# The gate products of a PEER layer: a scaled one-hot in two parts, two products a token

## The chip, the cores and the metric

The kernel runs on one core of one Trainium2 chip. The metric is the device time of one execution in microseconds (us). Three runs of the kernel before gave 2240.7, 2244.51 and 2245.97 us; their median, 2244.51 us, is the time to compare with. The execution that the profiler recorded took 2239.97 us.

## The reference

Two transformer blocks in fp32 follow each other: a hybrid mixer with a PEER feed-forward layer, then layers with attention and SwiGLU. The change touches the PEER layer alone. For each of 256 tokens and each of 8 heads it scores two sets of 128 sub-keys, takes the 16 best of each, adds them in pairs, keeps the 16 best sums, and reads from them 16 expert numbers out of 128 x 128 and 16 gates (a softmax). The result for a token is a sum over its 8 x 16 = 128 chosen experts:

```
u = w_down[ib]
act = gelu(einsum("td,thkd->thk", xb, u)) * gb
v = w_up[ib]
y = einsum("thk,thkd->td", act, v)
```

## The kernel before, in words

The kernel doesn't gather experts. It computes all 16384 of them for all 256 tokens and multiplies by a gate that is zero for experts that were not chosen. The experts stand as 128 rows (the first index) of 128 experts (the second index, on the partitions). For each row `r_` the loop in `peer` (from L963) multiplies 8 tiles of the down weights with the activations. Every weight tile and every activation is split into a high and a low part in fp32r, so a tile takes three one-pass products (`mm3`, L315 to L317): 24 products of 256 columns a row. The split of the weights runs on the way: ScalarE writes the high part wH (L288), and VectorE or, for every second group of four tiles, GpSimd writes the low part wL (L294). `self.share = 0.5` sets that half.

`value` puts the gelu of a row into `buf[:, r, n:]` (L957) for tokens whose gates are not there yet; for the first n tokens, which have their gates, it multiplies at once (L960, then L961 on GpSimd for odd rows and on VectorE for even ones).

`route` (a generator that the loop steps through) finds the experts of 128 tokens on VectorE. It ends with three transposes; `sel` then holds for each token the two indices of its 128 (head, choice) pairs on the partitions, and `gsel` their gates (L921, L922).

From row 60 on, each row also takes a group of four tokens. `onehot` (L928) builds, for both indices of the four tokens, one-hot matrices of 128 x 128 (L931, one VectorE instruction of 1024 columns, written over the tile `h`, which is parked in DRAM meanwhile) and scales the first of them by the gates: in one group of four by one VectorE instruction of 512 columns (L933), in the other three by four ScalarE instructions of 128 columns (L936). `gates` (L938) multiplies the two one-hots of each token in fp32 on TensorE (L943), which gives that token's 128 x 128 table of gates. The four tables lie interleaved in one PSUM bank (the token index is innermost). VectorE multiplies the rows that exist already into `buf` (L945), ScalarE copies the rest there (L947), where later rows find it. There are 64 groups, in rows 60 to 124.

Two buffers of one-hots (`oh[g % 2]`) let `onehot` run up to two groups ahead of the products. Within an engine the order of instructions is set by a planner that follows priorities and estimated durations, not by hand; semaphores carry what one engine needs of another.

After the 128 rows, the loop from L1001 multiplies with the up weights (L999); at `r == 4` of it the parked `h` comes back by DMA (L1013, L1014) and a factor `rn` of the next norm is computed (L1020).

Of the kernel before, what the change touches and what calls it, by code (L numbers as in the profile page):

```python
# [8 lines left out]
F32 = mybir.dt.float32  # L9
F32R = mybir.dt.float32r  # L10
I32 = mybir.dt.int32
U32 = mybir.dt.uint32
AF = mybir.ActivationFunctionType
ALU = mybir.AluOpType
# [4 lines left out]
P = 128  # L19
D = 1024  # L20
KD = D // P
S = 256
M = 16
T = M + S
# [183 lines left out]
class Net:  # L208
    def __init__(self, tc, ctx, I, out, dump=None):
        self.tc, self.nc, self.I, self.out = tc, tc.nc, I, out  # L210
        self.dump = dump or (lambda name, ap: None)
        nc = self.nc
        self.per = ctx.enter_context(tc.tile_pool(name="per", bufs=1))
        self.wp = ctx.enter_context(tc.tile_pool(name="wp", bufs=1))
        self.tp = ctx.enter_context(tc.tile_pool(name="tp", bufs=1))
        self.dr = ctx.enter_context(tc.tile_pool(name="dr", bufs=1, space=DRAM))
        per = self.per
        self.vecs = per.tile([P, NVEC], F32, name="vecs")
        nc.sync.dma_start(out=self.vecs[:, :KD], in_=I["vecs"][:, :KD])
        self.cst = per.tile([P, 7 * P], F32, name="cst")  # L220
        self.ident = self.cst[:, :P]
        self.tri = self.cst[:, P : 2 * P]
        self.tris = self.cst[:, 2 * P : 3 * P]
        self.blk = self.cst[:, 3 * P : 4 * P]
        self.iota = self.cst[:, 6 * P : 7 * P]
        self.band2 = self.cst[:, 4 * P + 64 : 4 * P + 64 + 32]
        self.band1 = self.cst[:, 5 * P : 5 * P + 31]
        self.halfm = self.cst[:, 5 * P + 64 : 5 * P + 66]
        self.ones = per.tile([P, P], F32, name="ones")
        nc.vector.memset(self.ones, 1.0)  # L230
        self.eps = {}
        for e in (1e-5, 1e-6):
            t = per.tile([P, 1], F32, name="eps%d" % len(self.eps))
            nc.vector.memset(t, e)
            self.eps[e] = t
        warm = per.tile([P, 1], F32, name="warm")
        nc.scalar.activation(out=warm, in_=self.eps[1e-5], func=AF.Sqrt)
        self.h = per.tile([P, KD, T], F32, name="h")
        self.uH = per.tile([P, KD, T], F32R, name="uH")
        self.uL = per.tile([P, KD, T], F32R, name="uL")  # L240
        self.nchunk = I["wall"].shape[0]
        self.raw = {}
        self.hl = {}
        self.loaded = 0
        self.split = 0
        self.pos = 0
        self.turn = 0.0
        self.share = 0.0
        self.factor = None
        self.over = ExitStack()  # L250
        self.later = []

    def behind(self, eng):

        return self.tc.issue_after(next(i for i in reversed(self.nc.cur_bb.bb.instructions) if i.engine == eng.engine))

    def vec(self, name, i=0, n=1):
        o, _ = VEC[name]
        return self.vecs[:, o + i : o + i + n]
# [536 lines left out]
    def peer(self):  # L796


        nc = self.nc
        h = self.h  # L800
        NT = P
        with ExitStack() as ctx:
            pool = ctx.enter_context(self.tc.tile_pool(name="pr", bufs=1))
            buf = pool.tile([P, NT, S], F32, name="buf")
            hd_ = self.dr.tile([P, KD, S], F32, name="hd")
            sel = pool.tile([P, S, 2], F32, name="sel")
            gsel = pool.tile([P, S], F32, name="gsel")

            rows = lambda a, b: buf[:, a:b].rearrange("p a b -> p (a b)")
            sc = rows(112, 128).rearrange("p (t m k) -> p t m k", t=2, k=P)  # L810
# [36 lines left out]
            for d in range(KD):  # L847
                t = self.t_("t", 2)[:, :S]
# [20 lines left out]
            def route(tt):  # L869
# [7 lines left out]
                for dst, src in ((cand, v), (cidx, fi)):  # L877
                    o = 0
                    for r0, r1, n in ((0, 1, 16), (1, 2, 8), (2, 4, 5), (4, 8, 3), (8, 16, 1)):
                        k = r1 - r0  # L880
                        nc.vector.tensor_tensor(
                            out=dst[:, :, o : o + k * n].rearrange("p h (a b) -> p h a b", b=n),
                            in0=src[:, :, 0, r0:r1, None].to_broadcast([P, 8, k, n]),
                            in1=src[:, :, 1, None, :n].to_broadcast([P, 8, k, n]), op=ALU.add)
# [31 lines left out]
                ts = slice(tt * P, (tt + 1) * P)  # L916
                p2 = self.bank("ax")
                nc.tensor.transpose(p2[:, :128], e[:, :128], self.ident)
                nc.tensor.transpose(p2[:, 128:256], e[:, 128:256], self.ident)
                nc.tensor.transpose(p2[:, 256:384], tv.rearrange("p h j -> p (h j)"), self.ident)  # L920
                nc.vector.tensor_copy(out=sel[:, ts].rearrange("p t i -> p i t"), in_=p2[:, :256].rearrange("p (i t) -> p i t", i=2))  # L921
                nc.vector.tensor_copy(out=gsel[:, ts], in_=p2[:, 256:384])  # L922
                yield

            flat = h.rearrange("p d t -> p (d t)")
            oh = [flat[:, 1024 * i : 1024 * (i + 1)].rearrange("p (t w k) -> p t w k", w=2, k=P) for i in range(2)]

            def onehot(g):  # L928
                o = oh[g % 2]
                ts = slice(4 * g, 4 * g + 4)  # L930
                nc.vector.tensor_tensor(out=o, in0=self.iota[:, None, None, :].to_broadcast([P, 4, 2, P]), in1=sel[:, ts, :, None].to_broadcast([P, 4, 2, P]), op=ALU.is_equal)  # L931
                if g % 4 == 0:
                    nc.vector.tensor_tensor(out=o[:, :, 0], in0=o[:, :, 0], in1=gsel[:, ts, None].to_broadcast([P, 4, P]), op=ALU.mult)  # L933
                else:
                    for t in range(4):
                        nc.scalar.activation(out=o[:, t, 0], in_=o[:, t, 0], func=AF.Copy, scale=gsel[:, 4 * g + t : 4 * g + t + 1])  # L936

            def gates(g, R):  # L938

                o = oh[g % 2]  # L940
                ps = self.bank("acc").rearrange("p (i t) -> p i t", t=4)
                for t in range(4):
                    nc.tensor.matmul(ps[:, :, t], o[:, t, 1], o[:, t, 0], start=True, stop=True)  # L943
                ts = slice(4 * g, 4 * g + 4)
                nc.vector.tensor_tensor(out=buf[:, :R, ts], in0=ps[:, :R], in1=buf[:, :R, ts], op=ALU.mult)  # L945
                if R < NT:
                    nc.scalar.activation(out=buf[:, R:, ts], in_=ps[:, R:], func=AF.Copy)  # L947

            pace = 0.0
            work = [x for tt in range(2) for x in [route(tt)]]  # L950
            done = 0
            pend = -1
# [35 lines left out]
            def act(r):  # L988
                i = r % LAST if r < N0 else LAST + r - N0
                t = self.uH[:, i, M:], self.uL[:, i, M:]  # L990
                self.hilo(*t, buf[:, r])
                acts[r] = t

            def add(r, d):
                H, L = self.wtile()
                o = y[d // 2][:, (d % 2) * S : (d % 2 + 1) * S]
                aH, aL = acts[r]
                for i, (a, b) in enumerate(((H, aH), (H, aL), (L, aH))):
                    nc.tensor.matmul(o, a, b, start=(r == 0 and d % 2 == 0 and i == 0), stop=(r == NT - 1 and i == 2), skip_group_check=True)  # L999
                return o  # L1000
# [4 lines left out]
            for r in range(N0):  # L1005
                if r + 2 < N0:
                    act(r + 2)
                if N0 - 3 * LAST <= r < N0 and (N0 - r) % 3 == 0:
                    act(NT - (N0 - r) // 3)
                for d in range(KD):  # L1010
                    add(r, d)
                if r == 4:
                    nc.scalar.dma_start(out=h[:, :, M:], in_=hd_)  # L1013
                    nc.scalar.dma_start(out=h[:, :, :M], in_=self.I["mt2"])  # L1014
                    w2 = pool.tile([P, KD], F32, name="w2")
                    nc.vector.tensor_tensor(out=w2, in0=self.vec("norm_fin", 0, KD), in1=self.vec("ln_ffn1_0", 0, KD), op=ALU.mult)
                    self.norm_begin("ln_ffn1_0", 0, M)
                    for d in range(KD):
                        self.norm_tile(d)
                    rn = self.norm_end(1e-6, self.t_("rnext", 1))  # L1020

# [5 lines left out]
            for d in range(KD):  # L1029
                for r in range(N0, NT):  # L1030
                    ps = add(r, d)
                o = h[:, d, M:]
# [554 lines left out]
```

## Time and profile before

| what | value |
|---|---|
| median of three runs | 2244.51 us |
| the profiled execution | 2239.97 us |
| span of its instructions | 2238.0 us |
| mean granted TensorE clock | 0.995 of full |
| TensorE busy (matmul rows) | 2169.0 us, 97% |
| VectorE busy | 1590.4 us, 71% |
| ScalarE busy | 1323.0 us, 59% |
| GpSimd busy | 671.7 us, 30% |

The span runs from the first instruction to the last; some 2 us of the execution's time lie around it. Busy times are averages over stages with different limits, so a single stage has to be read by itself: the stage of the gates lies between about 516 and 757 us of the span. In the rows, PE is TensorE's matmul, PEld its weight load, DVE is VectorE, ACT ScalarE, POOL GpSimd. A record's duration contains its latency, so neighbouring records on PE and DVE overlap, and the distance from start to start tells what one of them costs in a dense stretch.

### The profile page before, as it was taken

To read this page: it belongs to the slowest core of one execution; us is meant where nothing else is said; L and a number is where in the kernel's file an instruction comes from. 1 tells how busy PE (TensorE), PEld (TensorE's weight loads), DVE (VectorE), ACT (ScalarE), POOL (GpSimd) and SP (SyncE) were. 2 spreads that over 40 slices of the span, in tenths; PEclk is the share of its full clock that TensorE was granted. 3 is DMA by queue.
4 is the path that set the end of the run, shared out by engine and by line. 5 is a ranking of instruction groups with operands and counts; after the bars stand their busy time and mean duration, and the time that the engine had idled before them with its cause. 6 is when DMAs were issued, how large, how long until landed. Compare 5 with 4: busy or idle time off the path is not lost.

```text
span 2238.0 us, 45779 instructions
## 1 busy us (share of the span) xinstructions
PE 2169.0 (97%) x17351; PEld 2096.4 (94%) x17351; DVE 1590.4 (71%) x3143; ACT 1323.0 (59%) x2857; POOL 671.7 (30%) x567
## 2 busy tenths in 40 slices
PE   8998998899999999999999999999999999899999
PEld 7987998899999999999999998899999999679999
DVE  8889789955778766666586655876656666877664
ACT  8776654556766755555565555765555555666553
POOL 6684744444555400000031114122201211512220
PEclk9999999999999999999999999999999999999999
DMA  4523644454444555555565554145555555204555
GB/s 170 166 97 133 201 148 142 154 186 151 142 136 139 181 189 188 186 184 188 186 207 188 179 168 144 58 150 173 178 179 170 177 174 187 76 29 128 192 183 169
DMA packets 103948, 356.59 MB, mean 159 GB/s; under 512 B 12416, under 2 KB 20016, under 8 KB 103344
## 3 DMA queue, kind: packets, MB, share of 16 engines
q1 hardware_dynamic: 100096, 346.06, 46.8%
q10 hardware_dynamic: 3632, 7.62, 1.1%
q8 instruction: 136, 2.23, 0.4%
q14 instruction: 84, 0.69, 0.1%
HBM read 351.51 MB, written 5.40 MB: 159 GB/s over the span
## 4 chain that ended last, share of the span: by engine, by line
PE 76%; DVE 14%; ACT 5%; issue 3%; POOL 1%; DMA 1%; DVEq 0%; SPq 0%; ACTq 0%; POOLq 0%
PE acc L999 16%; PE mm L317 13%; PE mm L315 13%; PE mm L316 13%; PE acc L317 4%; PE acc L315 4%; PE acc L316 4%; DVE wL L294 3%; DVE h L931 2%; ACT h L936 1%; ACT wH L288 1%; DVE acc L526 1%; PE mm L1461 1%; PE acc L1485 1%; PE acc L943 1%
## 5 line engine op out<-in xcount | busy, mean ns | idle before, releaser
L288 ACT ACTIVATE wH<-raw 128x512 fp32r<-128x512 f32 x1296 | 806.6, 628 | 559.9 <-PE mm L316 237.8
L294 DVE TENSOR_TENSOR wL<-raw,wH 128x512 fp32r<-128x512 f32 x1037 | 756.3, 731 | 381.0 <-ACT wH L288 358.7
L317 PE MATMUL mm<-uH,wL 128*128 128x256 f32 (+1 forms) x2168 | 620.1, 286 | 19.9 <-DVE wL L294 19.2
L315 PE MATMUL mm<-uH,wH 128*128 128x256 f32 (+1 forms) x2168 | 628.3, 290 | 9.9 <-ACT wH L288 7.0
L316 PE MATMUL mm<-uL,wH 128*128 128x256 f32 (+1 forms) x2168 | 618.9, 286 | 2.4 <-DVE uL L359 2.3
L294 POOL TENSOR_TENSOR wL<-raw,wH 128x512 fp32r<-128x512 f32 x259 | 383.4, 1485 | 462.9 <-ACT wH L288 354.0
L317 PEld LDWEIGHTS mm<-uH,wL 128*128 128x128 f32 x2168 | 411.0, 190 | 24.7 <-DVE wL L294 23.8
L315 PEld LDWEIGHTS mm<-uH,wH 128*128 128x128 f32 x2168 | 410.9, 190 | 15.5 <-ACT wH L288 8.7
L316 PEld LDWEIGHTS mm<-uL,wH 128*128 128x128 f32 x2168 | 410.7, 189 | 5.9 <-DVE uL L359 4.2
L999 PE MATMUL acc<-uH,wH 128*128 128x256 f32 x1024 | 288.4, 282 | 1.7 <-DVE h L1033 1.1
L999 PE MATMUL acc<-uL,wH 128*128 128x256 f32 x1024 | 287.7, 281 | 0.4 <-DVE uL L357 0.4
L999 PE MATMUL acc<-uH,wL 128*128 128x256 f32 x1024 | 287.2, 281 | 0.0
L1086 POOL TENSOR_TENSOR t<-t,g 128x272 f32<-128x272 f32 (+1 forms) x88 | 108.2, 1231 | 415.6 <-ACT wH L288 326.2
L317 PE MATMUL acc<-uH,wL 128*128 128x272 f32 (+1 forms) x728 | 209.4, 288 | 0.0
L315 PE MATMUL acc<-uH,wH 128*128 128x272 f32 (+1 forms) x728 | 209.1, 287 | 0.0
L316 PE MATMUL acc<-uL,wH 128*128 128x272 f32 (+1 forms) x728 | 208.7, 287 | 0.0
L317 PE MATMUL mm<-gH,wL 128*128 128x272 f32 (+1 forms) x704 | 199.9, 284 | 0.0
L315 PE MATMUL mm<-gH,wH 128*128 128x272 f32 (+1 forms) x704 | 199.9, 284 | 0.0
L316 PE MATMUL mm<-gL,wH 128*128 128x272 f32 (+1 forms) x704 | 199.8, 284 | 0.0
L999 PEld LDWEIGHTS acc<-uH,wH 128*128 128x128 f32 x1024 | 194.1, 190 | 2.5 <-DVE h L1033 1.5
L999 PEld LDWEIGHTS acc<-uL,wH 128*128 128x128 f32 x1024 | 193.1, 189 | 0.6 <-DVE uL L357 0.6
L999 PEld LDWEIGHTS acc<-uH,wL 128*128 128x128 f32 x1024 | 193.0, 189 | 0.0
(400 smaller groups left out, 3918.0 us busy)
## 6 DMA issues: line engine op xcount, KB each, us to landing
raw<-in_wall_dram SPq DMA_DIRECT2D x648, 512.0 KB, 3.3
bdram<-brow ACTq DMA_DIRECT2D x1, 3200.0 KB, 13.7
b<-bdram SPq DMA_DIRECT2D x8, 272.0 KB, 4.6
b<-bdram SPq DMA_DIRECT2D x8, 144.0 KB, 4.2
buf<-in_keys_dram ACTq DMA_DIRECT2D x1, 1024.0 KB, 6.4
hd<-h ACTq DMA_DIRECT2D x1, 1024.0 KB, 5.4
h<-hd ACTq DMA_DIRECT2D x1, 1024.0 KB, 6.4
uv<-in_uv_dram ACTq DMA_DIRECT2D x1, 1024.0 KB, 5.8
```

The lines of the kernel that those rows point to most:

```text
L288: nc.scalar.activation(out=H, in_=w, func=AF.Copy)
L294: eng.tensor_tensor(out=L, in0=w, in1=H.bitcast(F32), op=ALU.subtract)
L315: mm(ps, H, xH, start=(k == 0), stop=False)
L316: mm(ps, H, xL, start=False, stop=False)
L317: mm(ps, L, xH, start=False, stop=(k == kt - 1))
L526: nc.vector.scalar_tensor_tensor(out=acc, in0=src, scalar=w, in1=acc, op0=ALU.mult, op1=ALU.add)
L931: nc.vector.tensor_tensor(out=o, in0=self.iota[:, None, None, :].to_broadcast([P, 4, 2, P]), in1=sel[:, ts, :, None].to_broadcast([P, 4, 2 ...
L936: nc.scalar.activation(out=o[:, t, 0], in_=o[:, t, 0], func=AF.Copy, scale=gsel[:, 4 * g + t : 4 * g + t + 1])
L943: nc.tensor.matmul(ps[:, :, t], o[:, t, 1], o[:, t, 0], start=True, stop=True)
L999: nc.tensor.matmul(o, a, b, start=(r == 0 and d % 2 == 0 and i == 0), stop=(r == NT - 1 and i == 2), skip_group_check=True)
L1086: nc.gpsimd.tensor_tensor(out=t, in0=t, in1=s, op=ALU.mult)
L1461: nc.tensor.matmul(ps[:, :nk], qa[hh][:, k, a : a + n], ckv[:, k, :nk], start=(k == 0), stop=(k == 1))
```

## The change

- The scaled one-hot is now made in two parts. The gates are split into `gselH` (rounded to fp32r) and `gselL` (the rest), and each part gives its own scaled one-hot, in one VectorE instruction per token and part with two scalars read per partition: compare with the index, multiply by the gate. ScalarE and L933 have no part in it any more. The plain one-hot of the second index is made for four tokens in one instruction of 512 columns into a new tile `hot2`.
- The product of a token in fp32 becomes two accumulating products in fp32r of 128 columns with the same stationary `hot2`.
- A token's table lies contiguous in PSUM; VectorE and ScalarE read it through a view with the token innermost.
- `sel`, `gselH` and `gselL` live in buffers of existing tags; `rn` too; the one-hots take the place of `h` as a tile of their own.

```diff
-        self.h = per.tile([P, KD, T], F32, name="h")
+        self.h = self.rows_()
...
+    def rows_(self):
+        return self.per.tile([P, KD, T], F32, name="h", tag="h", bufs=1)
...
-            sel = pool.tile([P, S, 2], F32, name="sel")
-            gsel = pool.tile([P, S], F32, name="gsel")
+            hot2 = pool.tile([P, 2, 4, P], F32R, name="hot2")
+            sel = [self.t_("g", 2)[:, :S] for _ in range(2)]
+            gselH = self.t_("ssq", 2, dt=F32R)[:, :S]
+            gselL = self.t_("ssq", 2)[:, :S]
...
-                nc.vector.tensor_copy(out=sel[:, ts].rearrange("p t i -> p i t"), in_=p2[:, :256].rearrange("p (i t) -> p i t", i=2))
-                nc.vector.tensor_copy(out=gsel[:, ts], in_=p2[:, 256:384])
+                for i in range(2):
+                    nc.vector.tensor_copy(out=sel[i][:, ts], in_=p2[:, i * P : (i + 1) * P])
+                nc.vector.tensor_copy(out=gselH[:, ts], in_=p2[:, 256:384])
+                nc.vector.tensor_tensor(out=gselL[:, ts], in0=p2[:, 256:384], in1=gselH[:, ts].bitcast(F32), op=ALU.subtract)
...
-            flat = h.rearrange("p d t -> p (d t)")
-            oh = [flat[:, 1024 * i : 1024 * (i + 1)].rearrange("p (t w k) -> p t w k", w=2, k=P) for i in range(2)]
+            gates_ = self.per.tile([P, KD * T], F32R, name="gates", tag="h", bufs=1)
+            oh = [gates_[:, 1024 * i : 1024 * (i + 1)].rearrange("p (w t k) -> p w t k", w=2, k=P) for i in range(2)]
...
-                nc.vector.tensor_tensor(out=o, in0=self.iota[:, None, None, :].to_broadcast([P, 4, 2, P]), in1=sel[:, ts, :, None].to_broadcast([P, 4, 2, P]), op=ALU.is_equal)
-                if g % 4 == 0:
-                    nc.vector.tensor_tensor(out=o[:, :, 0], in0=o[:, :, 0], in1=gsel[:, ts, None].to_broadcast([P, 4, P]), op=ALU.mult)
-                else:
-                    for t in range(4):
-                        nc.scalar.activation(out=o[:, t, 0], in_=o[:, t, 0], func=AF.Copy, scale=gsel[:, 4 * g + t : 4 * g + t + 1])
+                nc.vector.tensor_tensor(out=hot2[:, g % 2], in0=self.iota[:, None, :].to_broadcast([P, 4, P]), in1=sel[1][:, ts, None].to_broadcast([P, 4, P]), op=ALU.is_equal)
+                for t in range(4):
+                    c = slice(4 * g + t, 4 * g + t + 1)
+                    for w, part in ((0, gselH.bitcast(F32)), (1, gselL)):
+                        nc.vector.tensor_scalar(out=o[:, w, t], in0=self.iota, scalar1=sel[0][:, c], scalar2=part[:, c], op0=ALU.is_equal, op1=ALU.mult)
...
-                ps = self.bank("acc").rearrange("p (i t) -> p i t", t=4)
+                pt_ = self.bank("acc").rearrange("p (t i) -> p t i", t=4)
+                ps = pt_.rearrange("p t i -> p i t")
                 for t in range(4):
-                    nc.tensor.matmul(ps[:, :, t], o[:, t, 1], o[:, t, 0], start=True, stop=True)
+                    for w in range(2):
+                        nc.tensor.matmul(pt_[:, t], hot2[:, g % 2, t], o[:, w, t], start=(w == 0), stop=(w == 1))
...
+                    h = self.h = self.rows_()
...
-                    rn = self.norm_end(1e-6, self.t_("rnext", 1))
+                    rn = self.norm_end(1e-6, self.t_("rstd", 2))
```

## Rows read from the trace of the kernel before

**Rows 1.** Busy time by stretch: us, then PE, PEld, DVE, ACT, POOL, granted clock, DMA.

```profile
412.00:516.00 104.00, 98.47 (x822) 97.25 (x821) 67.30 (x138) 54.86 (x109) 51.85 (x35) 1.00 0.53 173
516.00:757.00 241.00, 240.73 (x2055) 239.85 (x2054) 182.34 (x237) 162.95 (x505) 125.92 (x95) 1.00 0.43 141
```

**Rows 2.** Groups of instructions in 516 to 757 us: busy, mean ns, idle before.

```profile
L294 POOL TENSOR_TENSOR wL<-raw,wH 128x512 fp32r<-128x512 f32 x64 | 111.8, 1747 | 108.9 <-ACT wH L288 90.7 <-DVE wL L294 9.7 <-PE acc L943 6.3
L931 DVE TENSOR_TENSOR h<-cst,sel 128x1024 f32<-128x1024 f32 x62 | 77.3, 1247 | 0.0
L943 PE MATMUL acc<-h 128*128 128x128 f32 x512 | 68.2, 276 | 0.3 <-DVE h L933 0.2
L936 ACT ACTIVATE h<-h,gsel 128x128 f32<-128x128 f32 x188 | 63.1, 393 | 25.9 <-DVE h L931 25.4
L294 DVE TENSOR_TENSOR wL<-raw,wH 128x512 fp32r<-128x512 f32 x64 | 48.9, 764 | 9.0 <-ACT wH L288 7.5 <-ACT buf L947 0.7 <-POOL buf L961 0.6
L945 DVE TENSOR_TENSOR buf<-acc,buf 128x248 f32<-128x248 f32 (+31 forms) x64 | 34.7, 542 | 33.5 <-ACT buf L957 30.6 <-ACT h L936 1.6 <-ACT t L960 1.2
L933 DVE TENSOR_TENSOR h<-h,gsel 128x512 f32<-128x512 f32 x15 | 25.5, 1698 | 0.3
```

**Rows 3.** Chain that ended last, 680 to 757 us: start, us, what.

```profile
700.58 0.89 PE acc L943 x8
...
753.38 0.89 PE acc L943 x8
```

**Rows 4.** Timeline of PE around one group of gates: start, us, engine, line.

```profile
643.42 1.05 PE L943 MATMUL acc<-h 128*128 128x128 f32 x8
...
644.43 0.28 PE L316 MATMUL mm<-uL,wH 128*128 128x256 f32 x1
644.55 0.28 PE L317 MATMUL mm<-uH,wL 128*128 128x256 f32 x1
```

**Rows 5.** Timeline of PEld: four loads of 128 columns for products of 8 columns.

```profile
1909.25 0.52 PEld L1385 LDWEIGHTS ax<-cst,wix 8*128 8x128 f32 x4 [0.36 <-issue]
1909.79 0.19 PEld L316 LDWEIGHTS mm<-qL,wH 128*128 128x128 f32 x1
```

**Rows 6.** DVE groups by form over the whole span, then a timeline of DVE.

```profile
L1474 DVE TENSOR_SCALAR lg<-lg,st 128x272 f32<-128x272 f32 x16 | 5.7, 354 | 0.2
L1474 DVE TENSOR_SCALAR lg<-lg,st 128x144 f32<-128x144 f32 x16 | 4.6, 285 | 0.0
L526 DVE SCALAR_TENSOR_TENSOR acc<-cin,vecs,acc 128x256 f32<-128x256 f32 x176 | 79.4, 480 | 2.1 <-PE acc L507 0.6
L357 DVE TENSOR_TENSOR uL<-buf,uH 128x256 fp32r<-128x256 f32 x128 | 53.1, 418 | 0.1
...
374.10 0.22 DVE L910 TENSOR_SCALAR buf<-buf 128x128 int32<-128x128 int32 x1
374.24 0.22 DVE L911 TENSOR_SCALAR buf<-buf 128x128 int32<-128x128 int32 x1
```

**Rows 7.** DVE and POOL against each other: two lines' durations (min/median/max ns), timelines.

```profile
L933 DVE TENSOR_TENSOR h<-h,gsel x16: 671/1666/1780, 422.0 to 740.1; 128x512 f32<-128x512 f32 x16
L1133 DVE TENSOR_SCALAR rq<-rq x3: 178/186/2053, 1399.5 to 1995.1; 128x24 f32<-128x24 f32 x2, 128x48 f32<-128x48 f32 x1
...
601.87 1.22 DVE L931 TENSOR_TENSOR h<-cst,sel 128x1024 f32<-128x1024 f32 x1
603.12 1.65 DVE L933 TENSOR_TENSOR h<-h,gsel 128x512 f32<-128x512 f32 x1
604.70 0.68 DVE L294 TENSOR_TENSOR wL<-raw,wH 128x512 fp32r<-128x512 f32 x1
...
602.01 2.22 POOL L294 TENSOR_TENSOR wL<-raw,wH 128x512 fp32r<-128x512 f32 x1 [0.91 <-DVE wL L294]
...
1949.91 7.05 POOL L1423 TENSOR_TENSOR b<-b,wk 128x2176 f32<-128x2176 f32 x1 [2.87 <-DVE wk L1417]
1954.95 2.05 DVE L1133 TENSOR_SCALAR rq<-rq 128x24 f32<-128x24 f32 x1
```

## The prediction

> **What bounds the kernel now.** I read the page first: TensorE is busy nearly everywhere, so the question is what TensorE spends on gates and who could hold it up. The table of stretches isolates the gates, 516 to 757 us: TensorE is busy 240.7 of 241 us at full clock (2.4 GHz), VectorE 182.3, ScalarE 163.0, GpSimd 125.9 [rows 1]. TensorE is the bound, and VectorE, with 58.7 us unspent, is next. The chain of waits for the second half of the stretch consists of products alone, with the eight gate records of a row at 0.89 us; from 700.58 to 753.38 us there are 14 rows, so a row takes 3.77 us [rows 3]. The timeline shows the same: gates from 643.42, and L316 at 644.43 where 643.54 would have been its place in an undisturbed beat of 0.12 us [rows 4]. The groups of the stretch then give what VectorE does in a row [rows 2].
>
> **TensorE's part.** An fp32 product of a token stands as two records (512 for 256 tokens [rows 2]), eight a row, 0.89 us. After, there are again eight passes a row: four tokens, two fp32r products each. What one costs isn't in the trace, since every fp32r product there moves 256 columns or more. If only moved columns counted, 128 would take half of the 0.12 us beat: 8 x 0.06 = 0.48, which saves 0.41 us a row, 26 us over 64 rows. But each product also loads 128 stationary columns, and products with the same stationary operand one after the other (L315 and L316, both wH) load it twice, one PEld record each. The row nearest to that limit is L1385: its products move 8 columns, and its four loads still start (0.52 - 0.19) / 3 = 0.11 us apart [rows 5]. Eight such loads are 0.88 us. I take this end: the load is as wide, and an fp32r load (the L316 behind them) lasts 0.19 us like these. So TensorE gains 0.01 us a row, nothing that counts. The other end is a short fp32r product that runs at fp32's price, two passes each: 16 x 0.11 = 1.76, a loss of 0.87 us a row, 56 us. That a table now lies contiguous in PSUM I take as free on all three engines; the loads' beat of 0.11 already accounts for the interleaved products, so there is nothing left to win there, and VectorE reads at one column a cycle from a broadcast view as from a plain one (L931, 1024 columns, 1.22 us at best). The bound above is that VectorE reads the table at half its rate, some 0.4 us a row, which goes into the range.
>
> The Trainium skill, "TensorE: Matmul & The Clock Gate", section "Back-to-back issue gap", gives 81 ns for a load and a product of 128 columns in a stream. By it eight would take 0.65 us, 0.24 less a row, 15 us less in all.
>
> **VectorE's part.** Starts lie about 0.08 us closer than durations: two neighbouring 128-column instructions of 0.22 us start 0.14 apart [rows 6].
> - Removed: L931, 62 in the stretch x (1.247 - 0.08) = 72.4 us, and L933, 15 x (1.698 - 0.08) = 24.3 us [rows 2]. VectorE is left with 182.3 - 96.7 = 85.6 us.
> - Added, `hot2`: 512 columns where L931 has 1024. L931 undisturbed takes 1.22 us [rows 7], a wL of 512 columns 0.68 [rows 7]; start to start 0.60. 64 x 0.60 = 38.4 us.
> - Added, eight tensor-scalar instructions of 128 columns a row, 512 in all. L1474, with one scalar read per partition, takes 285 ns for 144 columns and 354 for 272, so 0.54 ns a column and 276 ns for 128; less 0.08 is 0.195 [rows 6]. The new ones read two such scalars. One costs L526 over L357 480 - 418 = 62 ns at 256 columns, so the second costs between nothing and 0.06. I take the middle, 0.225 us: 115.2 us; the ends are 99.8 and 130.6.
> - Sum: 85.6 + 38.4 + 115.2 = 239.2 us, ends 223.8 and 254.6, in a stretch of 241. VectorE is full before it has waited for anyone.
>
> **What VectorE loses to GpSimd.** The two exclude each other on instructions that need two reads of SBUF. L933 takes 0.67 us once and 1.67 in the median; in the timeline a wL on GpSimd, issued at 602.01, can't proceed until L931 ends at 603.09, then runs 1.14 us to 604.23, and L933, started at 603.12, ends 0.54 us behind it [rows 7]. So whoever comes second waits for the whole of the other, about 1.0 us net. The tensor-scalar form is subject to it too: L1133 takes 0.19 us, and 2.05 when L1423 holds GpSimd [rows 7]. Today this costs VectorE 15 x 1.0 for L933 and some 0.08 on each wL (0.764 in the mean [rows 2] against 0.68 [rows 7]), about 0.3 us a row, because it has three such instructions a row and is idle for a quarter of the time. After, it has ten, back to back, and GpSimd still has one wL a row and every other L961. The lower end is no further loss; the upper end is 1.0 us for every row, 64 us. I take 0.6 a row, twice today's loss for a queue that is occupied throughout: 38 us. The Trainium skill, "SBUF — State Buffer", section "Who interferes with whom", makes this an exclusive lock for the whole instruction, tensor-scalar included; by it the upper end would hold, 64 us, and the kernel would stand near 2302 us.
>
> **ScalarE's part.** It sheds L936, 63.1 us of 163.0 [rows 2], and now has 100 us of 241. It is not the bound, so this buys nothing by itself; L945 will wait less for L957 (30.6 us now), which is what lets VectorE run full.
>
> **What else moves.** The route's end gains two short VectorE instructions per 128 tokens, where VectorE has 67 of 104 us busy [rows 1]: nothing. No DMA is added. `h` comes back when the last gates have been multiplied, as now, and `rn` only changes its buffer: nothing. The planner reorders queues by its own estimates; I allow 5 us either way.
>
> **The sum.** Stretch after: 239.2 + 38 = 277 us, against 241: +36 us. The profiled execution took 2239.97, so 2276; the median of the runs shown is 4.5 us above that execution, so I put the forecast 2 us higher, 2278 us. With GpSimd's loss full and scalars dear it is 254.6 + 64 - 241 = +78, 2318. What is late then is wL: TensorE's loads stand behind it, and behind the one-hots, a row at a time.
>
> **Rivals.**
> - *It fits.* Scalars read in parallel (0.195) and GpSimd's work falls where VectorE waits: 223.8 us plus a few, under 241. TensorE stays the bound at 3.77 us a row: 2240 to 2244 us. For it: 16 L933s that now come late in each fourth row go. Against: ten port instructions a row leave little room.
> - *Faster.* The load of a stationary fp32r operand hides behind the product before, the 0.06 end holds, and VectorE fits: TensorE would save 26 us, but VectorE's 223.8 stops it at 17, so about 2223 to 2227 us. It decides only if a product of 128 columns starts less than 0.11 us after its neighbour. Against: L1385's loads. By the 81 ns of the Trainium skill (page and section above) it would be 15 us.
> - *The change doesn't give one-pass products.* Below 256 columns fp32r would take fp32's two passes: +56 us on TensorE, with VectorE's 277 hidden under it, since a row would take 4.6 us: about 2297 us. Nothing in the trace shows such a product; nothing excludes it.
>
> **Chances.** Forecast 0.54, two passes 0.12, fits 0.19, faster 0.15. Slower gets the first two and the upper edge of the third, 0.67; within 0.2% (4.5 us, about what a measurement can tell from no change) 0.18; faster 0.15. The forecast's own range is 2255 to 2318. The 8-in-10 range adds the case that fits, 2238 to 2316, and leaves out the faster case and the very end above.
>
> **What would show it.** Right: in the stretch of the gates (longer than 241 us) VectorE busy over 95%, TensorE's idle time ended by wL and by the new tensor-scalar line, tensor-scalars of 0.3 us with some of over 1 us, L943's eight records still 0.85 to 0.9 us a row, ScalarE down by some 60 us. Wrong: TensorE busy throughout as now (it fits); gate records 0.06 to 0.08 us apart (faster); 16 or more records a row, or eight that are 0.2 apart (two passes).

## The result, and the profile after

The kernel after takes 2318.01 us (median of four runs, 2312.7 to 2321.23) against 2242.61 us for the kernel before beside it: a ratio of 1.0332 (95% interval 1.0309 to 1.0354), 75 us slower. The forecast, 2278 us, had the sign and the mechanism; the time lies 2 us beyond the range. The profiled executions stand a little further apart than the medians: 2321.23 against 2239.97 us.

The first view is the busy time in the stretch of the gates, with the columns of [rows 1].

```profile
518.00:830.00 312.00, 269.38 (x2068) 253.73 (x2067) 308.51 (x718) 106.88 (x322) 97.14 (x96) 0.99 0.34 111
```

Where TensorE was busy for 240.7 of 241 us, it is now busy for 269 of 312, and VectorE, 182 before, for 308.5 of 312. The granted clock stayed at 0.99 of 2.4 GHz, so TensorE's clock doesn't explain it. ScalarE fell from 163 to 107 us, which buys nothing. From the first gate product to the last, 237.5 us became 305.4. The whole span grew by 81.4 us: 2.4 ahead of the gates, 67.9 in them, 11.2 behind them. The last of these three nobody expected; it has its own part below.

The groups of the stretch name the line (busy, mean ns, idle before, as in [rows 2]; L943 is now the tensor-scalar, L952 the gate product, L297 wL, L939 `hot2`, L954 what L945 was).

```profile
L943 DVE TENSOR_SCALAR gates<-cst,g,ssq 128x128 fp32r<-128x128 f32 x496 | 206.2, 475 | 1.6 <-PE acc L952 1.6
...
L952 PE MATMUL acc<-gates,hot 128*128 128x128 f32 x512 | 90.6, 283 | 42.6 <-DVE gates L943 42.0
L297 POOL TENSOR_TENSOR wL<-raw,wH 128x512 fp32r<-128x512 f32 x64 | 83.3, 1302 | 214.1 <-ACT wH L291 132.6 <-DVE gates L943 42.7 <-PE mm L319 35.3
...
L297 DVE TENSOR_TENSOR wL<-raw,wH 128x512 fp32r<-128x512 f32 x64 | 44.2, 690 | 1.3 <-ACT wH L291 1.3
L939 DVE TENSOR_TENSOR hot<-cst,g 128x512 fp32r<-128x512 f32 x62 | 41.9, 676 | 0.0
```

L943 has no idle time before it (1.6 us): it works or is held up inside its own records. TensorE's idle time is put down to it, 42 us at the gate products. L943's mean of 475 ns hides two kinds of record, and another view, all durations of one line (min/median/max), parts them:

```profile
L943 DVE TENSOR_SCALAR gates<-cst,g,ssq x512: 326/336/1464, 422.7 to 823.8; 128x128 fp32r<-128x128 f32 x171
```

Half last 336 ns or less; 86 of the 512 last more than 400 ns, 74 of these more than 600 and 64 more than 1000, as many as there are wL on GpSimd, and what the 86 lie above 336 adds up to 71 us. One row in the timeline shows where that comes from:

```profile
643.80 2.58 DVE L943 TENSOR_SCALAR gates<-cst,g,ssq 128x128 fp32r<-128x128 f32 x6
...
644.18 0.75 PEld L952 LDWEIGHTS acc<-gates,hot 128*128 128x128 f32 x6
644.22 1.31 POOL L297 TENSOR_TENSOR wL<-raw,wH 128x512 fp32r<-128x512 f32 x1 [3.08 <-ACT wH L291]
...
645.67 0.44 PEld L952 LDWEIGHTS acc<-gates,hot 128*128 128x128 f32 x2 [0.73 <-DVE gates L943]
...
646.30 0.68 DVE L297 TENSOR_TENSOR wL<-raw,wH 128x512 fp32r<-128x512 f32 x1
```

Six tensor-scalars would take some 1.6 us and take 2.58, with GpSimd's wL (644.22 to 645.53) in the midst of them (one such hold-up is called a block below); at 645.67, right behind its end, TensorE gets the last two loads of its group. Six of those loads in 0.75 us, each 0.19 long, start (0.75 - 0.19) / 5 = 0.11 us apart: the price that L1385 gave [rows 5].

### The profile page after: what moved, and what is told of

Its sections match the earlier page's. It is cut to its first block, busy times and chain, and to the rows that moved or that the text cites. A ratio compares the mean times of both kernels' runs of the same rounds, so it can differ in the third digit from the quotient of the medians.

```text
span 2319.4 us, 46257 instructions
## 1 busy us (share of the span) xinstructions
PE 2203.7 (95%) x17351; PEld 2115.4 (91%) x17351; DVE 1715.5 (74%) x3643; ACT 1264.1 (55%) x2665; POOL 639.8 (28%) x567
## 4 chain that ended last, share of the span: by engine, by line
PE 74%; DVE 18%; issue 4%; ACT 3%; POOL 1%; DMA 0%; DVEq 0%; SPq 0%; ACTq 0%; POOLq 0%
PE acc L1008 15%; PE mm L318 13%; PE mm L320 13%; PE mm L319 13%; DVE gates L943 5%; PE acc L320 4%; PE acc L318 4%; PE acc L319 4%; DVE wL L297 3%; PE acc L952 1%; DVE acc L529 1%; DVE hot L939 1%; PE mm L1471 1%; PE acc L1495 1%; DVE buf L954 1%
## 5 line engine op out<-in xcount | busy, mean ns | idle before, releaser
L297 DVE TENSOR_TENSOR wL<-raw,wH 128x512 fp32r<-128x512 f32 x1037 | 749.7, 724 | 379.1 <-ACT wH L291 360.9
L319 PE MATMUL mm<-uL,wH 128*128 128x256 f32 (+1 forms) x2168 | 619.6, 286 | 2.2 <-DVE uL L362 2.0
L297 POOL TENSOR_TENSOR wL<-raw,wH 128x512 fp32r<-128x512 f32 x259 | 353.0, 1367 | 574.9 <-ACT wH L291 399.1
L319 PEld LDWEIGHTS mm<-uL,wH 128*128 128x128 f32 x2168 | 410.5, 189 | 5.6 <-DVE uL L362 4.0
L943 DVE TENSOR_SCALAR gates<-cst,g,ssq 128x128 fp32r<-128x128 f32 x512 | 212.7, 474 | 1.6 <-PE acc L952 1.6
L319 PE MATMUL acc<-uL,wH 128*128 128x272 f32 (+1 forms) x728 | 209.0, 287 | 0.0
L319 PE MATMUL mm<-gL,wH 128*128 128x272 f32 (+1 forms) x704 | 202.5, 288 | 0.0
```

Source lines behind the costliest of these rows:

```text
L297: eng.tensor_tensor(out=L, in0=w, in1=H.bitcast(F32), op=ALU.subtract)
L319: mm(ps, H, xL, start=False, stop=False)
L943: nc.vector.tensor_scalar(out=o[:, w, t], in0=self.iota, scalar1=sel[0][:, c], scalar2=part[:, c], op0=ALU.is_equal, op1=ALU.mult)
```

## The experiments

**Who holds VectorE up.** Two kernels move GpSimd's half of wL from row 60 on: all to VectorE, or all to GpSimd.

```diff
             for r_ in range(NT):
+                self.share = 0.5 if r_ < 60 else 0.0   # e5_all_pool: 1.0
```

> From row 60 on GpSimd makes no wL any more, VectorE makes them all. Theory (VectorE is the bound of the stage, and one wL on GpSimd a row blocks it for about 1.1 us): VectorE takes 0.61 us a row more for the second wL and loses 1.1 us less, so 64 x 0.5 = 32 us are won back: about 2286 us against 2318 of the changed kernel, and tensor-scalars of over 1 us vanish from the stage. Rival (VectorE simply has too much work and the long tensor-scalars wait for something else): 64 x 0.61 = 39 us more, about 2357 us, with the long ones still there.

> The kernel after, with both wL of a row on GpSimd from row 60 on (the mirror of e1_no_pool). Theory (whoever comes second waits for the whole of the other): VectorE is relieved of one wL a row, 0.61 us, and is held up a second time, another 1.1 us; 64 rows x 0.5 = +31 us in the stage of the gates, about 2349 us. Rival (the blocks are a matter of how much work VectorE has, not of how often GpSimd holds the port): VectorE sheds 64 x 0.61 = 39 us, about 2279 us. Nothing of the computation changes.

e1_no_pool took 2295.28 us, ratio 1.0241 (1.0224 to 1.0258); e5_all_pool 2345.23 us, 1.0467 (1.0451 to 1.0482), 4 us from the theory and 66 from its rival. The groups of the gates' stretch, first of e1_no_pool, then of e5_all_pool:

```profile
L943 DVE TENSOR_SCALAR gates<-cst,g,ssq 128x128 fp32r<-128x128 f32 x496 | 146.2, 343 | 0.2 <-PE acc L952 0.2
L297 DVE TENSOR_TENSOR wL<-raw,wH 128x512 fp32r<-128x512 f32 x131 | 88.6, 678 | 2.5 <-ACT wH L291 2.5
```

```profile
L943 DVE TENSOR_SCALAR gates<-cst,g,ssq 128x128 fp32r<-128x128 f32 x495 | 265.4, 600 | 0.0
L297 POOL TENSOR_TENSOR wL<-raw,wH 128x512 fp32r<-128x512 f32 x130 | 167.4, 1307 | 156.9 <-ACT wH L291 64.5 <-PE acc L952 51.9 <-issue 34.9
```

Without GpSimd's wL the mean of L943 is 343 ns, close to its median of 333 (10 records over 600 ns); with two a row it is 600. More work on VectorE made the kernel faster, less work made it slower. The price comes out the same both ways. In e1_no_pool the stage lasts 277.7 us, 27.6 less than after, although VectorE took over 64 wL at 0.61 = 39 us; so the 64 blocks had cost 66 us. In e5_all_pool it lasts 330.2 us, 24.8 more, although VectorE shed 39; 64 more blocks cost 64. One wL on GpSimd costs a full VectorE 1.0 us. The rule of the Trainium skill, "SBUF — State Buffer", "Who interferes with whom", by which the second one waits for the whole of the first, agrees: of such a wL's 1.3 us by its record, VectorE loses 1.0.

**What a second scalar costs.** The multiplier becomes a constant.

```diff
-scalar2=part[:, c], op0=ALU.is_equal, op1=ALU.mult)
+scalar2=1.0, op0=ALU.is_equal, op1=ALU.mult)
```

> The changed kernel with the constant 1.0 in place of the second scalar of the eight tensor-scalars (left out: the gates' weights). Theory (the second scalar read per partition costs 0.06 us each, which is why they start 0.257 us apart and not 0.195): 512 x 0.06 = 31 us less, about 2287 us, tensor-scalars of 0.28 us. Rival (the second scalar is free and the long start-to-start distance is the fp32r output's or another fixed cost): 2318 us as before, tensor-scalars of 0.336 us.

It took 2298.2 us, 1.0261 (1.0243 to 1.0279). All durations of L943 in e4_one_scalar:

```profile
L943 DVE TENSOR_SCALAR gates<-cst,g x512: 268/275/1408, 421.7 to 799.3; 128x128 fp32r<-128x128 f32 x171
```

275 ns instead of 336; from start to start of undisturbed neighbours 0.196 us in the median instead of 0.257. The second scalar costs 0.061 us, all of what L526 over L357 had shown [rows 6] and not the half that I took. 512 x 0.061 = 31 us, of which the stage gained 22.5. The blocks stayed (77 records over 600 ns) and cost more: what the held-up records take beyond an undisturbed distance adds up to 76 us, against 69 in the kernel after.

**TensorE's part by itself.** The one-hots are built for the first two groups only, in the kernel after and in the kernel before, so that nothing but the products bounds the stage.

```diff
-                        onehot(pend)
+                        if pend < 2:
+                            onehot(pend)
```

> The changed kernel with the one-hots of groups 0 and 1 alone; the other 62 groups multiply those again (left out: their own one-hots). Theory (the products cost TensorE what the fp32 ones did, because each loads 128 stationary columns at 0.11 us): TensorE is the bound at 3.75 us a row, 2236 to 2246 us. Rival one (a product of 128 moved columns takes half a beat, 0.06 us): 26 us under the kernel before, about 2216 us. Rival two (short fp32r products are themselves slow, and VectorE's queue only looks like the cause): 2290 us or more.

> The kernel before with the one-hots of groups 0 and 1 alone (left out: the other 62). It gives TensorE's own time with fp32 products. Theory: it was TensorE's already, apart from every fourth row, where L933 came some 0.2 us late: 2237 to 2242 us. If the one-hots of the kernel before still cost something hidden, it is under 2232 us.

e2_after_hot_once took 2246.71 us, 1.0022 (1.0012 to 1.0032), e3_before_hot_once 2239.73 us, 0.9999 (0.9989 to 1.0008). The stretch of the gates in e2_after_hot_once, columns of [rows 1], then the timeline of PEld and PE around one of its groups:

```profile
516.00:757.00 241.00, 241.00 (x2081) 241.00 (x2080) 80.73 (x161) 119.77 (x323) 102.87 (x97) 1.00 0.45 145
...
644.73 0.97 PEld L952 LDWEIGHTS acc<-gates,hot 128*128 128x128 f32 x8
...
644.85 1.00 PE L952 MATMUL acc<-gates,hot 128*128 128x128 f32 x8
...
645.86 0.28 PE L319 MATMUL mm<-uL,wH 128*128 128x256 f32 x1
```

TensorE is full again, and from the first to the last gate product the stage takes 234.4 us, against 236.0 in e3_before_hot_once. Hardly any of these 1.6 us is the gate products' own: from the first product of a group to the second product behind it (L319 here, L316 in [rows 4]) it is 1.011 us in the median here and 1.013 in e3_before_hot_once, 0.1 us over 64 groups. The rest lies in the rows' other products, which start 117.3 instead of 118.3 ns apart in the mean; why is open. So two products in fp32r cost what one in fp32 did. The loads are what is paid: eight of them start (0.97 - 0.19) / 7 = 0.11 us apart. The Trainium skill's 81 ns ("TensorE: Matmul & The Clock Gate", "Back-to-back issue gap"), 15 us less by the prediction, is not what these products showed: their median start to start is 111 ns. One distance in each of the 64 groups is about 58 ns, that from the first product to the second. So products of 128 columns can start that close; the group gains nothing by it, since the loads keep their distance.

But then e2_after_hot_once should have been a little faster than e3_before_hot_once, and it was 7 us slower. That is the surprise.

**The 8 us behind the gates.** Page rows of one group of the ffn layers' second products (busy, mean ns), in the kernel before, then in the kernel after:

```profile
L315 PE MATMUL mm<-gH,wH 128*128 128x272 f32 (+1 forms) x704 | 199.9, 284 | 0.0
```

```profile
L318 PE MATMUL mm<-gH,wH 128*128 128x272 f32 (+1 forms) x704 | 202.5, 288 | 0.0
```

The change doesn't touch these products (gH and gL are the high and the low part of the layer's gated activations, their moving operand), nothing makes them wait, and their loads, columns and clock (1.00 of full) are the same. Yet each starts later behind the one before it (this distance is called the beat here): 126.66 instead of 123.33 ns in the mean at 272 columns (some 1584 products), 118.66 instead of 113.37 at 256 (some 528). That is 5.3 + 2.8 = 8.1 us. What did change is where gH and gL lie. When `rn` moved to the tag `rstd`, the tag `rnext` went away, and all that is allocated behind it lies 272 floats lower. `ffn` begins with an unused tile, `gpad`, which sets the place of gH. One kernel puts gH back in the kernel after; one moves it by 64 bytes in the kernel before, and both are edits of one number:

```diff
-            pool.tile([P, 112], F32, name="gpad")
+            pool.tile([P, 384], F32, name="gpad")   # e6_after_as_before; 96 in e7_before_pad
```

> The kernel after, with the unused tile ahead of gH in the ffn raised from 112 to 384 floats a partition: the 272 floats that the tag rnext took in the kernel before, so gH and gL lie where they lay there. Theory (the slower beat of the products with gH and gL is a matter of where these tiles lie): 272-column products go from 126.7 back to 123.3 ns and 256-column ones from 118.7 to 113.4, about 8 us less, 2310 us, and the stage of the gates stays as long as in the kernel after (305 us between its first and last product). Rival (something else of the change, such as the h tile made anew, slows them): the beats stay and so does the time, 2318 us. Nothing of the computation changes.

> The kernel before, with the unused tile ahead of gH lowered from 112 to 96 floats a partition, so gH and gL lie 64 bytes lower and all else stays. Theory of placement, if a step of 64 bytes is what counts (the kernel after lies 1088 bytes lower, 17 such steps): the beats of before rise to 126.7 and 118.7 ns and the time by 8 us, about 2250 us. Rival (placement does nothing, or only a larger offset does): the time of the kernel before, 2240 to 2243 us, and beats of 123.3 and 113.4 ns. Nothing of the computation changes.

e7_before_pad took 2249.4 us, 1.0037 (1.0023 to 1.0051): 16 floats of an unused tile cost 8 us. e6_after_as_before took 2312.39 us, 1.0326 (1.031 to 1.0342); its interval overlaps with that of the kernel after, so here the trace has to speak. The same page row, in e7_before_pad, then in e6_after_as_before:

```profile
L315 PE MATMUL mm<-gH,wH 128*128 128x272 f32 (+1 forms) x704 | 202.8, 288 | 0.0
```

```profile
L318 PE MATMUL mm<-gH,wH 128*128 128x272 f32 (+1 forms) x704 | 199.9, 284 | 0.0
```

The beats are exchanged, to the digit: 126.66 and 118.66 ns in e7_before_pad, 123.33 and 113.37 in e6_after_as_before. In the latter the stage of the gates is as long as in the kernel after (305.4 us), and the span from the last up product to the end is 8.6 us shorter. So the place costs 8 us; of the 11.2 behind the gates, 3 remain without a cause.

**Is it a rule?** In the kernel before, gH and gL begin 192 bytes behind a multiple of 256; in the kernel after and in e7_before_pad, 128. The lines of uH and uL are 1088 bytes long, so their place changes from line to line. One kernel gives the rows' activations lines of 1024 bytes at 192:

```diff
+            pH, pL = [x.rearrange("p d t -> p (d t)")[:, 48 : 48 + KD * S].rearrange("p (d t) -> p d t", t=S) for x in (self.uH, self.uL)]
+            pu = lambda k: (pH[:, k], pL[:, k])
...
-                self.hilo(self.uH[:, d, M:], self.uL[:, d, M:], t)
+                self.hilo(*pu(d), t)
...
-                self.linear(1, KD, self.u(M, T), S, lambda m, ps: value(r_, ps))
+                self.linear(1, KD, pu, S, lambda m, ps: value(r_, ps))
```

> The kernel before, with the activations of the 128 rows (uH, uL) stored in lines of 1024 bytes that begin 192 bytes behind a multiple of 256, where gH and gL lie in the kernel before, instead of lines of 1088 bytes, whose place changes from line to line. It tries whether what e6_after_as_before and e7_before_pad showed for gH and gL holds for any moving operand. Theory (the place of the moving operand in 256 bytes sets the beat): the 3072 products of the rows go from 118.2 to 113.4 ns, 15 us less, about 2227 us. Rival (it takes something more, as the up products suggest, whose third line in four lies at such a place and has a beat of 113 ns in the first eight rows only and 118 later): the beat stays near 118 and the time at 2241 us. Nothing of the computation changes.

2239.58 us, 0.999 (0.998 to 1.0). Neither theory holds whole: the beat of the rows' products went from 118.2 ns in the mean to 115.7, of two kinds, about half at 113.4 and half at 117.9. Mostly all products of a row are of one kind, and in the stage of the gates rows of the two kinds take turns for long. The stage still took 237.3 us, although the beat gave it some 3 us, in part because TensorE's loads waited 3.4 us, instead of 1.0, for the one-hot that VectorE scales in every fourth group. That the place of a moving operand can set the beat is shown for gH and gL; what else it takes for a beat of 113 ns is open.

**A version that fits.** If blocks by GpSimd are the cause, the same products should cost nothing once VectorE issues few instructions that can be blocked. e8_scalar_H returns the scaling of the high part to ScalarE and leaves the low part on VectorE in three groups of four; gH lies as before.

```diff
-                    for w, part in ((0, gselH.bitcast(F32)), (1, gselL)):
-                        nc.vector.tensor_scalar(out=o[:, w, t], in0=self.iota, scalar1=sel[0][:, c], scalar2=part[:, c], op0=ALU.is_equal, op1=ALU.mult)
+                    nc.scalar.activation(out=o[:, 0, t], in_=hot1[:, t], func=AF.Copy, scale=gselH.bitcast(F32)[:, c])
+                    if g % 4 == 0:
+                        nc.scalar.activation(out=o[:, 1, t], in_=hot1[:, t], func=AF.Copy, scale=gselL[:, c])
+                if g % 4:
+                    nc.vector.tensor_tensor(out=o[:, 1], in0=hot1, in1=gselL[:, ts, None].to_broadcast([P, 4, P]), op=ALU.mult)
```

> The kernel after with gH and gL placed as before and the one-hots made another way: two VectorE compares of 512 columns a row (the first into a bf16 tile), the high part scaled by four ScalarE instructions a row, the low part by one VectorE multiply of 512 columns in three rows of four and by four ScalarE instructions in the fourth. Theory: VectorE has 1.34 + 2 x 0.60 + 0.75 x 0.62 = 3.0 us a row and some 0.3 to 0.6 of blocks by GpSimd, ScalarE 1.67 + 5 x 0.33 = 3.3 us, both under TensorE's 3.66 us (e2_after_hot_once), so TensorE bounds the stage again: 2246.7 - 8 = about 2238 us, at best 4 us under the kernel before. Rival: with four port instructions a row VectorE is blocked for the full 1.1 us a row and for its own waits on ScalarE, 4.1 us a row, 28 us more, about 2266 us. Nothing of the computation changes.

2263.18 us, 1.0099 (1.0084 to 1.0114): near the rival. Its stretch of the gates in the busy time by stretch:

```profile
518.00:778.00 260.00, 252.34 (x2065) 244.04 (x2063) 240.68 (x326) 194.00 (x622) 117.09 (x97) 1.00 0.41 132
```

And all durations of its compare of the first index, L941:

```profile
L941 DVE TENSOR_TENSOR rstd<-cst,g x64: 677/1580/1601, 410.1 to 760.5; 128x512 bf16<-128x512 f32 x64
```

VectorE is at 93%, and its instructions are fewer, but the median L941 lasts 1580 ns where it could last 677: 44 of the 64 last over 1 us, held up by GpSimd's wL, 0.9 us each time. Averaged over the 64 rows, 0.6 us, that is the upper end of the 0.3 to 0.6 us that I had taken, and L297 on VectorE (1018 ns in the mean, 690 in the kernel after) has blocks of its own on top: the same step as in the prediction. The next kernel takes the wL from GpSimd and moves half of the low part to ScalarE:

```diff
-                    if g % 4 == 0:
+                    if g % 2 == 0:
...
-                if g % 4:
+                if g % 2:
...
+                self.share = 0.5 if r_ < 60 else 0.0
```

> e8_scalar_H without its blocks: from row 60 on no wL on GpSimd, and the low part scaled by ScalarE in every second row instead of every fourth. Theory (in e8_scalar_H VectorE, 93% busy, was the bound again because of the port, about 0.9 us a row): VectorE has 1.34 + 1.20 + 0.31 + 0.61 = 3.5 us a row and a block only by L976 on every second row, ScalarE 1.67 + 6 x 0.32 = 3.6, TensorE 3.66: the stage takes 235 to 245 us and the kernel 2238 to 2250 us. Rival (the chain from the compare on VectorE over ScalarE and VectorE to the product is what is too long, not the sum of VectorE's work): the stage stays at 255 us and the kernel near 2263 us. Nothing of the computation changes.

2239.75 us, 0.9992 (0.9982 to 1.0001), as the theory had it. The stretch of the gates in e10_no_pool_scalar_H, and then all durations of L941:

```profile
517.00:755.00 238.00, 238.00 (x2056) 238.00 (x2055) 217.64 (x378) 214.09 (x691) 21.87 (x31) 1.00 0.43 143
```

```profile
L941 DVE TENSOR_TENSOR rstd<-cst,g x64: 679/693/1765, 412.2 to 742.4; 128x512 bf16<-128x512 f32 x64
```

L941's median is 693 ns, TensorE is busy throughout, the stage takes 234.4 us, and VectorE and ScalarE, 91 and 90% busy, fit under it. This kernel changes two things at once, but L941 itself shows that its blocks are gone. With the products of the change the kernel now stands where it stood without them; 2 us between the medians are too little for these runs to tell. A group takes 1.011 us here too, so only 0.1 us of them could be the gate products' own. The last kernel puts both together, the change that fits and the placed activations:

> e10_no_pool_scalar_H with the activations of the rows placed as in e9_before_u_placed. If the two gains are of separate work and add, 1.5 to 2 us for the cheaper gate products and 2 to 3 us for the lines of the activations, the kernel takes about 2237 us and is the first that beats the kernel before (by 0.2%). If the products of the rows were held up by something else in e9_before_u_placed and gain nothing, it stays at 2240 us. Nothing of the computation changes.

2235.64 us, 0.9976 (0.9964 to 0.9988): the time fell by about the sum of the two gains, and this version beats the kernel before by 5 us and the kernel after by 82. Its stage of the gates takes 229.9 us, with TensorE full, 7.6 less than in the kernel before, where e9_before_u_placed had gained 0.3 and e10_no_pool_scalar_H 3.1. The rows' products there now nearly all have the faster beat, 113.7 ns in the mean:

```profile
513.00:751.00 238.00, 238.00 (x2097) 237.87 (x2096) 219.81 (x380) 215.79 (x696) 20.72 (x32) 1.00 0.45 147
```

## Why the prediction was right in kind and 40 us short

**TensorE's part** was right. The load of 128 columns, 0.11 us, sets the price of a short product; eight passes a row cost what they did, and neither the gain at 0.06 nor the loss at two passes came. The row that carried it was a far one [rows 5], and it held. The gain of 0.01 us a row was 0.002.

**VectorE's own work** was right in sum by luck, through two errors of opposite sign. Predicted: 115.2 for the tensor-scalars, 38.4 for `hot2`, 85.6 for the rest, 239.2 us. In e1_no_pool, by distances from start to start: 132.0 (6 of it blocks that were left), 37.1, and 108.7 less the 39 us of wL added there = 69.7; in sum 238.8. The tensor-scalars were too cheap because of the second scalar, taken at half of its 0.06. The rest was too dear, as I read it, because I took its busy time, while for the new instructions I subtracted the 0.08 us by which neighbours overlap; for its 160 instructions that is 13 of the 16 us.

**What VectorE loses to GpSimd** is the step that failed: "I take 0.6 a row, twice today's loss for a queue that is occupied throughout: 38 us." It is 1.0 us a row, 66 us, the upper end. The row of one collision [rows 7] had the price right; what I mis-sized is how often it is paid. For an idle quarter of the time a block costs VectorE nothing that anybody waits for. In a queue that is never empty, each wL on GpSimd meets a tensor-scalar (64 records of over 1 us for 64 wL), and each block is a loss. This is 28 of the 45 us between the sum for the profiled execution, 2276, and the 2321.23 it took.

**"`rn` only changes its buffer: nothing"** failed too, for 8 us. The buffer was nothing; that the tag it left went away moved every tile behind it, and with gH and gL 2112 products got a slower beat.

The remainder, some 9 us, are 3.5 from setting VectorE's 277 us against a stretch of 241 where the products' own stage is 237.5, 2.4 ahead of the gates, and the 3 us behind them that are left unexplained. That the prediction's upper sum, 2318 us, is the measured time is luck: it has VectorE's own work 16 us too dear and knows nothing of the 8 us of the place or of this remainder.

**What would show it** came in most points: VectorE at 99% in the stretch, TensorE's idle time ended by the tensor-scalar line, tensor-scalars of 0.33 us with some of over 1 us, ScalarE down by 56 us. wL, which was to end TensorE's idle time too, did not: no product or load of the rows waited. Gate products 0.06 us apart, named as a sign of the faster case, were there too, one pair in each group, and saved nothing.

## What to carry to other kernels

Cost an engine's new load at the rate of a full queue: a block by another engine that delays nobody while there is slack costs all of its 1.0 us here once the slack is gone, and moving work *onto* the full engine can then pay, as in e1_no_pool. Price a product of few columns by its load, not by its columns. And when a change frees or adds a buffer, compare the beat of untouched products before and after, since a tile that was moved by 64 bytes can cost as much as a term of the sum.

## What was not expected of the hardware

- The beat of fp32r products depends on where the moving operand lies: 113.37 or 118.66 ns at 256 columns, 123.33 or 126.66 at 272, for the same instructions with gH 64 bytes apart (e7_before_pad against before). It isn't settled where it has to lie: the third of four lines of the up products, also at 192 bytes, has 113 ns in the first eight rows and 118 later, and e9_before_u_placed got 113.4 in about half of the products and 117.9 in the others, mostly by whole rows.
- The Trainium skill, "TensorE: Matmul & The Clock Gate", "LDWEIGHTS (loading the stationary operand)", gives a load by its column count, 107 ns at 128 columns as an estimate by that page; the trace agrees, with 111 ns from load to load.
- A second per-partition scalar costs a tensor-scalar of 128 columns 0.061 us, as much as 113 columns at the 0.54 ns of [rows 6].
